# Wider spacing of the pieces of a recurrent layer between matrix products, on one Trainium2 core

## The chip, the cores and the metric

The kernel runs on one core of a Trainium2 chip. The metric is the device time of one execution in microseconds (us); the kernel before took 2150.6 us, the median of three runs (2145.4 to 2152.1). All engines below are those of the one core: PE (TensorE, matrix products and transposes), PEld (its loading of weights, which overlaps the products), DVE (VectorE), ACT (ScalarE), POOL (GpSimd) and SP (SyncE, which here issues the transfers).

## The reference

The program is a two-layer decoder trunk on 1024 tokens of width 1024, all in float32. The first layer mixes tokens by a gated linear recurrence (HGRN2), the second by attention in a sliding window of 128; each is followed by a gated feed-forward part with a short convolution (width 2816), and each part ends in `layer_norm(ALPHA * h + part)`. The change touches the recurrence. Cut to what matters, it is:

```python
q, f, i, g = jnp.split(h @ w_in, 4, axis=-1)            # w_in: 1024 x 4096, eight heads of 128
fg = lb + (1.0 - lb) * jax.nn.sigmoid(heads(f))
o = hgrn2_chunkwise(jax.nn.silu(heads(q)), 1.0 - fg, heads(i), jnp.log(fg))
    # S_t = diag(f_t) S_{t-1} + k_t v_t^T ;  o_t = S_t^T q_t
o = o * lax.rsqrt(jnp.mean(jnp.square(o), -1, keepdims=True) + RMS_EPS)
o = o * g_norm_w.astype(jnp.float32) * jax.nn.silu(heads(g))
return o.reshape(B, S, D).astype(h.dtype) @ w_out       # then layer_norm(ALPHA * x + ...)
```

So for each head there are four columns of projections (f, q, value, gate), a causal product whose scores carry the decay between two tokens, a state that is handed on from block to block of 128 tokens, a norm, a gate, and last the output projection over all heads.

## The kernel before, in words

**Arithmetic.** A float32 product is made of three fast ones, `mm3` (lines 173, 174, 175): each operand is split into a high part, which ACT casts (lines 154, 200, 811), and a low part, which DVE gets by a subtraction (line 147). Products with 512 columns into PSUM run back to back on PE for most of the program. PSUM holds four tiles `psmm` for the big products and two tiles `psax`, each of two banks, for everything else; whoever asks for a third `psax` waits until a tile has been read out.

**The stages.** (1) The input x comes in eight blocks of 128 tokens; PE turns each (`x_block`), ACT casts the high part, DVE subtracts, and ACT copies the turned block in full into the buffer `XF[tb]` for sums that are made later (lines 931 and 932). In between, the values of heads 0 and 1 and then the f, q and gate of head 0 are projected. (2) Thirteen "pairs" of columns (head 1's f and q, the gates of heads 1 and 2, f and q of head 2, the values of heads 2 and 3, and so on) are computed by a Strassen-like scheme: seven products of four `mm3` steps (twelve matmuls) each instead of eight (`product`), so 84 matmuls a pair. Three of the seven read sums of blocks of x (`SX`, called `sx` in the rows) on the right-hand side of SBUF, the others read `T` or sums in `HL`. The weights of each are loaded by SP, summed by DVE (lines 993 to 1009), and split. (3) Head 7's gate, the output projection (`out_part`, `out_proj`), the feed-forward part, then the second layer.

**The chain of a head.** While stage 2 runs, a generator `recur(h)` computes one head after the other in pieces. The pieces of a head are: on DVE the element-wise products r0, qp, r1 and r2 (lines 1187, 1188, 1190, 1194); on PE column sums of them and the first scores (line 179, tiles `St`, `kd`, `og`, `qp`, `kp`), which DVE places into `Ab` by mask (line 1141); scores over blocks of 8 and 16, with copies into `A` by ACT; wide scores over 32 and 64 tokens; the transposes of the keys (line 183, copied by ACT at line 1241); V times keys, which gives the states `St` (lines 1255, 1257); A times V plus states times q, then squares on ACT (line 1270), a power on POOL (lines 1271 and 1272) and the normed output `og` on DVE (line 1273); and the transposes of `og`, which DVE multiplies by the gate (line 1279) and SP writes to DRAM (`hod`). Between the scores, the queries and keys are scaled level by level (`update`): queries by DVE (line 1173), keys by POOL (line 1175) but for level 0, factors by DVE (line 1181). `turn_values` transposes the values of two heads (line 1124 is the copy).

**What sets the order.** PE and SP take their instructions in the order in which the program is written. The object `od` writes it: each `mm3` step advances a modelled clock, and each `yield n` in a generator means that its next piece is emitted when that clock has gone on by n us, so that matrix products lie between two pieces. DVE, ACT and POOL are ordered by a scheduler at build time; `urgent()` moves an instruction ahead there. A generator that waits on `state[...]` emits nothing until another has set it. What the yields are today, for heads 1 to 6:

```python
5.0   # og's transposes of the head before are out -> column sums and first scores
4.2   # -> scores over 8 and 16
4.2   # -> wide scores
2.2   # -> transposes of the keys
2.2   # -> V times keys
2.6   # -> A times V
8.0   # -> transposes of og
```

The time in the trace is not that of the model: on the chip one product of 512 columns follows the other after 0.22 to 0.23 us (the trace shows products at 219.80 and 220.02 us).

## Time and profile before

| | before |
|---|---|
| three runs | 2150.6, 2152.1, 2145.4 us |
| profiled execution: its time, its span | 2147.4 us, 2145.6 us |
| mean granted clock of PE | 0.996 |
| busy share: PE, PEld, DVE, ACT, POOL | 98%, 81%, 79%, 46%, 9% |
| recurrent layer with its heads | about 0 to 500 us |

The span runs from the first to the last instruction of the profiled execution. A timeline row gives start, duration, engine, line, operation, the tile written and the tile read, and in brackets the idle time ahead of it and what ended it. A row of the waits gives engine, tile, line, what was waited for, then total us, times, and the longest. A row of the windows gives the stretch, its length, busy time of each engine with the number of instructions, the granted clock (1.00 is full speed), the busy share of the DMA engines and GB/s.

### The profile page before, as it was taken

What the parts mean: (1) busy time and instruction counts of PE and PEld (TensorE: products, weight loads), DVE (VectorE), ACT (ScalarE), POOL (GpSimd) and SP (SyncE); (2) the same over time, 40 slices, a digit from 0 to 9 for tenths busy, and PEclk for the clock granted to TensorE, in tenths of its full rate; (3) what the DMA queues carried; (4) which work ended last, traced back from release to release, by engine and by line L of the source; (5) the groups of instructions that cost most, each with busy time, mean ns of one, the idle gap of its engine ahead of it and who ended that gap; (6) DMA issues with size and microseconds to landing.
All of it is one profiled execution on the core that took longest, in us unless ns stands there. A gap on an engine that the chain in (4) does not pass through costs nothing.

```text
span 2145.6 us, 32017 instructions
## 1 busy us (share of the span) xinstructions
PE 2104.6 (98%) x12511; PEld 1746.0 (81%) x12511; DVE 1690.5 (79%) x2282; ACT 994.5 (46%) x1586; POOL 202.6 (9%) x194
## 2 busy tenths in 40 slices
PE   9999999899999999999999999999999999999998
PEld 8888777778888888888888888888888888888886
DVE  6677666767988888887988546769988888887986
ACT  6454444442454444444433246743644444444430
POOL 1122122121100000000001123311000000000002
PEclk9999999999999999999999999999999999999999
DMA  4111111243243455547854311231244445559662
GB/s 152 40 50 48 33 50 54 76 152 108 98 130 110 147 164 167 167 138 268 301 192 167 116 35 36 62 138 72 85 158 138 154 144 163 167 170 314 229 225 99
DMA packets 268643, 285.25 MB, mean 133 GB/s; under 512 B 32073, under 2 KB 204874, under 8 KB 268234
## 3 DMA queue, kind: packets, MB, share of 16 engines
q1 hardware_dynamic: 267976, 283.06, 40.0%
q8 instruction: 98, 1.61, 0.3%
q14 instruction: 55, 0.45, 0.1%
q10 hardware_dynamic: 450, 0.12, 0.0%
q0 software_dynamic: 64, 0.02, 0.0%
HBM read 217.06 MB, written 66.09 MB: 132 GB/s over the span
## 4 chain that ended last, share of the span: by engine, by line
PE 75%; DVE 13%; DMA 7%; ACT 2%; issue 2%; SPq 1%; POOL 1%; DVEq 0%; ACTq 0%; POOLq 0%
PE psmm L173 15%; PE psmm L174 15%; PE psmm L175 15%; PE psax L173 8%; PE psax L175 7%; PE psax L174 7%; PE psax L179 3%; DVE HL L147 3%; DMA Y<-in_ffn_w_out_dram 2%; PE psmm L179 1%; PE psax L1528 1%; PE psax L183 1%; PE psmm L183 1%; DMA bsd<-Y 1%; DVE T L147 1%
## 5 line engine op out<-in xcount | busy, mean ns | idle before, releaser
L200 ACT CAST HL<-raw 128x1024 fp32r<-128x1024 f32 (+1 forms) x194 | 195.0, 1009 | 284.1 <-DVE raw L430 125.2
L173 PE MATMUL psmm<-T,HL 128*128 128x512 f32 x784 | 311.5, 397 | 0.9 <-ACT Y L494 0.8
L175 PE MATMUL psmm<-T,HL 128*128 128x512 f32 x784 | 305.9, 390 | 1.6 <-DVE HL L147 1.6
L174 PE MATMUL psmm<-T,HL 128*128 128x512 f32 x784 | 305.8, 390 | 0.1
L147 DVE TENSOR_TENSOR HL<-raw,HL 128x1024 fp32r<-128x1024 f32 (+1 forms) x218 | 258.5, 1189 | 56.1 <-ACT HL L200 28.6
L560 DVE SCALAR_TENSOR_TENSOR Y<-Y,cwt 128x1022 f32<-128x1022 f32 (+1 forms) x176 | 225.0, 1281 | 33.7 <-ACT Y L557 32.2
L222 POOL TENSOR_TENSOR rs<-rs,nhalf 128x1 f32<-128x1 f32 x32 | 46.0, 1439 | 1400.9 <-DVE rs L221 1400.9
L175 PEld LDWEIGHTS psmm<-T,HL 128*128 128x128 f32 x784 | 147.3, 188 | 33.7 <-DVE HL L147 2.1
L173 PEld LDWEIGHTS psmm<-T,HL 128*128 128x128 f32 x784 | 147.5, 188 | 32.0 <-ACT Y L494 2.1
L174 PEld LDWEIGHTS psmm<-T,HL 128*128 128x128 f32 x784 | 147.5, 188 | 29.7 <-DVE T L147 1.0
L173 PE MATMUL psax<-T,HL 128*128 128x512 f32 x352 | 137.9, 392 | 2.6 <-ACT Y L494 2.6
L175 PE MATMUL psax<-T,HL 128*128 128x512 f32 x352 | 137.1, 389 | 0.0
L174 PE MATMUL psax<-T,HL 128*128 128x512 f32 x352 | 137.0, 389 | 0.0
L557 ACT ACTIVATE Y<-Y,cwt 128x1024 f32<-128x1024 f32 x88 | 109.3, 1244 | 9.2 <-DVE Y L480 3.7
L454 DVE TENSOR_TENSOR Y<-Y 128x256 f32<-128x256 f32 x176 | 74.4, 423 | 44.7 <-DMA Y<-in_ffn_w_out_dram 42.7
L173 PE MATMUL psmm<-HL 128*128 128x512 f32 x216 | 86.7, 402 | 1.1 <-ACT G L1082 1.1
L174 PE MATMUL psmm<-HL 128*128 128x512 f32 x216 | 85.3, 395 | 0.0
L175 PE MATMUL psmm<-HL 128*128 128x512 f32 x216 | 85.2, 394 | 0.0
L173 PEld LDWEIGHTS psax<-T,HL 128*128 128x128 f32 x352 | 66.0, 188 | 17.5 <-ACT Y L494 4.1
L564 ACT ACTIVATE Y<-Y 128x1024 f32<-128x1024 f32 x44 | 46.5, 1061 | 71.2 <-DVE Y L560 71.2
L175 PEld LDWEIGHTS psax<-T,HL 128*128 128x128 f32 x352 | 66.1, 188 | 13.9
L174 PEld LDWEIGHTS psax<-T,HL 128*128 128x128 f32 x352 | 66.1, 188 | 13.5
(428 smaller groups left out, 5250.4 us busy)
## 6 DMA issues: line engine op xcount, KB each, us to landing
raw<-in_ffn_w_in_dram SPq DMA_DIRECT2D x136, 256.0 KB
raw<-gd SPq DMA_DIRECT2D x118, 256.0 KB
gd<-Y SPq DMA_DIRECT2D x44, 512.0 KB
Y<-in_ffn_w_out_dram SPq DMA_DIRECT2D x88, 256.0 KB
bsd<-Y SPq DMA_DIRECT2D x88, 256.0 KB
raw<-in_hgrn_w_in_dram SPq DMA_DIRECT2D x54, 256.0 KB
raw<-in_ffn_w_out_dram SPq DMA_DIRECT2D x54, 256.0 KB
R<-bsd SPq DMA_DIRECT2D x44, 256.0 KB
```

Source lines behind the costliest of these rows:

```text
L147: make = lambda e: e.tensor_tensor(lo, src, hi.bitcast(F32), op=ALU.subtract)
L173: nc.tensor.matmul(ps, st(0), mv(0), start=start, stop=False, **free)
L174: nc.tensor.matmul(ps, st(0), mv(1), start=False, stop=False, **free)
L175: nc.tensor.matmul(ps, st(1), mv(0), start=False, stop=stop, **free)
L179: nc.tensor.matmul(ps, lhsT, rhs, start=start, stop=stop, **kw)
L183: nc.tensor.transpose(ps, src, ident)
L200: nc.scalar.copy(hi, src)
L222: nc.gpsimd.tensor_tensor(rs, rs, nhalf, op=ALU.pow)
L454: tt(x, y, z, op=sub)
L557: nc.scalar.activation(c, u, AF.Identity, bias=cwt[:, l, 3, ci:ci + 1], scale=cwt[:, l, 2, ci:ci + 1])
L560: nc.vector.scalar_tensor_tensor(c[:, sh:], u[:, :S - sh], cwt[:, l, 2 - sh, ci:ci + 1], c[:, sh:], op0=ALU.mult, op1=ALU.add)
L564: nc.scalar.activation(c, c, AF.Silu)
```

## The change

The edits, in the order of the program:

- A tile `rpad` of 32 bytes in each partition is put first on the right-hand side of SBUF, so all that lies there (X, the sums SX, the tiles RA and Y) moves by 32 bytes: their addresses were 32 over a multiple of 64 and are now multiples of 64.
- While x is turned, the full copies of blocks 0 to 3 are made by DVE instead of ACT. Of blocks 4 to 7 ACT copies one half, and DVE makes the two sums of the block there (they were made later, at lines 931 and 932).
- The gates rotate through three tiles `gt0` to `gt2` instead of `Gx`, `G0`, `G1`.
- The yields between a head's pieces become a table `SP`; the pieces of `turn_values` come earlier (0.5, 1.5, and 1.5 more before the value counts as turned), and its copy and that of the keys are `urgent`.
- The transposes of the convolution's weights and the bias (`conv_params`) go into one `psax` tile and leave it in two copies; there were five tiles, each with its copy, with yields between them.
- The last head scales its keys on DVE, keeps r2 in a gate tile, and shares one `psax` tile from the transposes of the keys on; its first DVE pieces are emitted during head 6's last yield. The output projection's tiles 4 and 5, which lie in the other `psax`, begin once its wide scores are emitted (before: once its norm is). Tiles 0 to 3 of that projection go through heads 0 to 3 first and then heads 4 to 6; the heads' outputs 4 to 6 are loaded back later.

The diff, cut to its core:

```diff
+    ctx.enter_context(tc.tile_pool(name="rpad", bufs=1, side="right")).tile([P, 8], F32, name="rpad")
...
-                nc.scalar.copy(XF[tb], ps)
+                if tb < 4:
+                    copies[tb] = ps
+                    if tb:
+                        x_copy(tb)
+                else:
+                    a21, s1 = XF[tb][:, :512], XF[tb][:, 512:]
+                    nc.scalar.copy(a21, ps[:, :512])
+                    tt(s1, a21, ps[:, 512:], op=add)
+                    tt(a21, XF[tb - 4][:, :512], a21, op=sub)
+
+            copies = {}
+
+            def x_copy(tb):
+                nc.vector.tensor_copy(XF[tb], copies[tb])
...
                 us.append(split_into(hl_at(3), raw1).rearrange("p h (k c) -> p h k c", k=4))
+                x_copy(0)
...
             yield 12.0
-            for l, k, cr in crs:
-                ps = psax()
-                nc.tensor.transpose(ps[:, :88], cr, ident[:88, :88])
-                nc.vector.tensor_copy(cwt[:, l, 2 * k:2 * k + 2, :], ps[:, :88].rearrange("p (a b) -> p a b", a=2))
-                yield 1.0
             ps = psax()
-            nc.tensor.matmul(ps[:16, :2 * P], rb, oh, start=True, stop=True)
+            for i, (l, k, cr) in enumerate(crs):
+                nc.tensor.transpose(ps[:, 88 * i:88 * i + 88], cr, ident[:88, :88])
+            nc.tensor.matmul(ps[:16, 512:512 + 2 * P], rb, oh, start=True, stop=True)
+            nc.vector.tensor_copy(cwt.rearrange("p a b c -> p (a b c)"), ps[:, :4 * 88])
...
-            tt(s1, a21, s1, op=add)
-            tt(a21, a11, a21, op=sub)
...
-                    dest[n] = [hp.tile([P, S], F32, name=f"G{(h + i) % 2}") for i in range(2)]
+                    dest[n] = [hp.tile([P, S], F32, name=f"gt{(h + i) % 3}") for i in range(2)]
...
-                yield (0.5, 3.0)[e]
+                yield (0.5, 1.5)[e]
...
-                nc.scalar.copy(v, ps.rearrange("p (c t) -> p c t", c=NB))
+                with urgent():
+                    nc.scalar.copy(v, ps.rearrange("p (c t) -> p c t", c=NB))
+                yield 1.5
                 state["values"] = h + e
...
+            SP = {0: (7.5, 4.4, 4.4, 2.8, 2.8, 3.2, 8.0), NH - 1: (7.0, 4.2, 4.2, 2.4, 2.6, 2.6, 8.0)}.get(
+                h, (7.0, 5.0, 5.0, 2.8, 2.8, 3.2, 8.0))
...
+            def again():
+                if h < NH - 1:
+                    return psax()
+                if not kept:
+                    kept.append(psax())
+                return kept[0]
...
-                    (nc.gpsimd if i else nc.vector).tensor_tensor(view(nk, 0), view(k, 0),
+                    (nc.gpsimd if 0 < i and h < NH - 1 else nc.vector).tensor_tensor(view(nk, 0), view(k, 0),
...
-            yield {0: 7.5, NH - 1: 8.0}.get(h, 5.0)
+            yield SP[0]
...
-            nc.scalar.copy(kd, ps)
+            with urgent():
+                nc.scalar.copy(kd, ps)
...
-                yield from recur(h, *weights["out"].pop(h))
+                task = tasks.pop(h, None) or recur(h, *weights["out"].pop(h))
+                for wait in task:
+                    while h == NH - 2 and state["summed"] == h and wait > 0 and not tasks:
+                        if state["projected"] > h:
+                            tasks[h + 1] = recur(h + 1, *weights["out"].pop(h + 1))
+                            next(tasks[h + 1]), next(tasks[h + 1])
+                        else:
+                            yield 0.6
+                            wait -= 0.6
+                    yield wait
...
-        for tb in range(4):
-            begun.append(psmm())
-            out_part(begun[tb], us, tb, range(KC - 1))
+        begun = [psmm() for _ in range(4)]
+        for hs in (range(4), range(4, KC - 1)):
+            for tb in range(4):
+                out_part(begun[tb], us, tb, hs)
...
-        while state["summed"] < NH - 1:
+        while state["wide"] < NH - 1:
             od.step(chain)
```

How the change moves instructions is shown at three places. In the rows, a name with a number (`raw_92`) is one of several tiles of that name.

**DVE, where head 3 ends and head 4 begins.** The products that a head starts with (St, qp, kd, then og, which is r2) stand here behind the gating of the head before and behind low parts of weights (HL). Before:

```order
L1279 SCALAR_TENSOR_TENSOR G_2117<-psax,par,G_2117 128x1024
L147 TENSOR_TENSOR HL<-raw_92,HL 128x2x512
L1089 TENSOR_TENSOR qs<-qs,psmm 128x512
L147 TENSOR_TENSOR HL<-raw_93,HL 128x512
L1181 TENSOR_TENSOR tot<-tot 128x128
L1187 TENSOR_TENSOR St<-qs,kp 128x1024
L1188 TENSOR_TENSOR qp<-qs,fg 128x1024
L1181 TENSOR_TENSOR tot<-tot 128x64
L1190 TENSOR_TENSOR kd<-kp,qp 128x512
L997 TENSOR_TENSOR raw_93<-raw_92 128x512
L1173 TENSOR_TENSOR qp<-qp,fg 128x512
L1175 TENSOR_TENSOR kp<-kp,fg 128x512
```

And now:

```order
L1298 TENSOR_TENSOR og<-psax,ss 128x1024
L1210 TENSOR_TENSOR St<-qs,kp 128x1024
L1211 TENSOR_TENSOR qp<-qs,fg 128x1024
L1213 TENSOR_TENSOR kd<-kp,qp 128x512
L1196 TENSOR_TENSOR qp<-qp,fg 128x512
L1198 TENSOR_TENSOR kp<-kp,fg 128x512
L1304 SCALAR_TENSOR_TENSOR gt_2076<-psax,par,gt_2076 128x1024
L1217 TENSOR_TENSOR og<-kp,qp 128x512
L147 TENSOR_TENSOR HL<-raw_91,HL 128x2x512
L1096 TENSOR_TENSOR V<-V,psmm 128x512
```

The new head's first five operations stand directly behind the norm of the head before (line 1298, which was 1273) and ahead of its gating (line 1304, which was 1279).

**PE, the values of heads 6 and 7.** The eight transposes of a value (`ident,V`) and the seven products of values and keys (`V,kd`). Before:

```order
L175 MATMUL psmm<-sx_514,HL 128x512
L183 MATMUL psax<-ident,V 128x128 x8
L179 MATMUL psax<-V,kd 128x128 x7
L173 MATMUL psmm<-sx_514,HL 128x512
L174 MATMUL psmm<-sx_514,HL 128x512
```

And now:

```order
L179 MATMUL psax<-qp,kp 32x32 x32
L179 MATMUL psax<-St,kd 32x32 x32
L173 MATMUL psmm<-T,HL 128x512
L174 MATMUL psmm<-T,HL 128x512
L175 MATMUL psmm<-T,HL 128x512
L183 MATMUL psax<-ident,V 128x128 x8
L173 MATMUL psmm<-T,HL 128x512
```

The transposes stood directly ahead of the products that read their copy; they now stand behind the scores over 8 and 16, 27 matmuls of 512 columns or more ahead of those readers.

**ACT, at the start, while x is turned.** Casts of turned blocks (line 811, now 812), full copies (line 813) and the cast of the second half of the first weights (`HL<-raw_92`). Before:

```order
L833 COPY warm<-nhalf 128x1
L811 CAST T<-psax 128x8x128
L813 COPY kp<-psax 128x1024
L154 CAST HL<-raw_92 128x1024
L811 CAST T<-psax 128x8x128
L813 COPY og<-psax 128x1024
```

And now:

```order
L847 COPY warm<-nhalf 128x1
L812 CAST T<-psax 128x8x128
L154 CAST HL<-raw_92 128x1024
L812 CAST T<-psax 128x8x128 x3
L782 COPY V<-psmm 128x2x2x128
```

The cast of the weights now follows the first block's cast directly, and the full copies of the first four blocks are gone from ACT.

## The prediction

> **What bounds the kernel now.** I read the busy table of the page first, then PE's windows by stage, then PE's waits in the heads' stage, then the timeline around those waits.

> ```profile
> span 2145.6 us, 32017 instructions
> PE 2104.6 (98%) x12511; PEld 1746.0 (81%) x12511; DVE 1690.5 (79%) x2282; ACT 994.5 (46%) x1586; POOL 202.6 (9%) x194
> ```

> PE is busy for 98% of the span: over the whole only 41.0 us are idle, so a change that takes no PE work away can return little more than that, plus what the clock costs. The windows tell where the idle time lies (busy time, granted clock, DMA share, GB/s):

> ```profile
> 0.00:20.00 20.00, 16.04 (x108) 1.00 0.93 326
> 60.00:120.00 60.00, 59.10 (x546) 1.00 0.13 39
> 120.00:200.00 80.00, 78.35 (x907) 1.00 0.17 52
> 200.00:300.00 100.00, 93.65 (x966) 0.98 0.18 54
> 300.00:400.00 100.00, 92.46 (x790) 0.97 0.15 46
> 400.00:500.00 100.00, 94.89 (x918) 1.00 0.35 127
> ```

> From 60 to 500 us, where the heads run, PE is busy 418.45 of 440 us: 21.55 us idle, half of the program's. The clock is below 1.00 only in two of these windows. What the idle time of 60 to 500 us waited for (total, times, longest):

> ```profile
> PE psax L179 <- POOL kp L1175: 4.3, 3, 1.8
> PE psax L179 <- ACT V L1124: 4.0, 3, 1.7
> PE psax L179 <- DVE Ab L1141: 3.7, 4, 1.8
> PE psax L179 <- DVE og L1194: 2.6, 2, 1.6
> PE psax L907 <- DVE G L1279: 1.7, 1, 1.7
> PE psmm L175 <- DVE HL L147: 1.6, 1, 1.6
> PE psax L179 <- DVE tot L1181: 1.2, 1, 1.2
> PE psmm L173 <- ACT G L1082: 1.1, 1, 1.1
> PE psax L179 <- DVE qp L1173: 0.9, 1, 0.9
> ```

> These rows sum to 21.1 us, so they are nearly all of the idle time: each wait is a piece of a head that PE reaches before DVE, ACT or POOL has made its input. Every wait also costs a little more than it shows:

> ```profile
> 220.02 0.39 PE L174 MATMUL psmm<-T,HL 128*128 128x512 f32 x1
> 220.25 0.39 PE L175 MATMUL psmm<-T,HL 128*128 128x512 f32 x1
> 221.78 0.50 PE L173 MATMUL psmm<-HL 128*128 128x512 f32 x1 [1.15 <-ACT G L1082]
> ```

> One product lasts 0.39 us but the next begins 0.23 us after it, so each restart loses an overlap of 0.16 us that counts as busy.

> **The change, part by part.** The sum is made against the profiled execution, 2147.4 us (span 2145.6), 3.2 us under the median.

> *Pieces spread wider.* No PE work is added or removed by the yields; between a head's pieces there lie three matmuls more (0.68 us at 0.227 us each) ahead of the scores, the wide scores, and V times keys, and the column sums come 45 matmuls behind the last head's transposes (10.2 us) instead of 36 to 39 (8.2 to 8.9; heads 5 and 7 had 57). Further, DVE now makes the new head's r0, qp and r1 ahead of the gating of the last one and of low parts of weights, and so earlier against PE by those operations (the order of DVE shows them). The rows `kp`, `og` and `tot` (8.1 us) are at the sums and first scores; 1.3 to 2.0 us later and an earlier DVE cover waits of at most 1.8 us each. I leave 0.5 us at head 7, whose spacing of the scores stays 4.2: 7.6. `Ab` (3.7 us, four times, up to 1.8): the scores' 0.68 us and the wide scores' 0.68 us follow one another, so 1.36 us each, and I take 3.2. `V` (4.0 us): the transposes stood directly ahead of V times keys, or close to the wide scores; now 27 or more matmuls (6.1 us) lie between them and the copy's reader, and the longest wait was 1.7, so all 4.0 goes. `G L1279` (1.7) is a chain of five turned convolution weights through `psax`, now one: it goes. `G L1082` (1.1) is ACT's copy of a gate, held by the writing of that gate tile's last content to DRAM:

> ```profile
> 221.15 0.59 ACT L1082 COPY G<-psmm 128x512 f32<-128x512 f32 x1 [3.52 <-DMA hod<-G]
> ```

> With a third tile that transfer has another pair's time (84 matmuls, 19 us); it goes. Of `HL` (1.6 us, once) I take 1.0: DVE's queue is another there, and nothing was done for it. `qp` (0.9) stays: head 0's spacing ahead of its sums doesn't move. Sum: 7.6 + 3.2 + 4.0 + 1.7 + 1.1 + 1.0 = 18.6, and 15 restarts at 0.16 make 2.4: **-21.0 us** (0 to 24.1: all 21.55 and 16 restarts).

> *The clock.* Twice PE ran at half clock after two such waits in a row:

> ```profile
> 277.95 0.64 PE L179 MATMUL psax<-og,one 128*32 128x256 f32 x8 [1.05 <-DVE og L1194]
> 279.82 1.08 PE L179 MATMUL psax<-qp,kp 128*32 128x32 f32 x64 [1.23 <-DVE tot L1181]
> ...
> 337.04 0.64 PE L179 MATMUL psax<-og,one 128*32 128x256 f32 x8 [1.58 <-DVE og L1194]
> 338.91 1.08 PE L179 MATMUL psax<-qp,kp 128*32 128x32 f32 x64 [1.23 <-POOL kp L1175]
> ...
> 279.90:283.10 3.20, 3.20 (x69) 0.50 0.02 5
> 338.00:344.00 6.00, 5.09 (x74) 0.50 0.01 3
> ```

> Half of the busy time of these stretches is the loss, (3.20 + 5.09) / 2 = 4.1 us at most. Both stretches begin behind waits of 2.3 and 2.8 us in all, and from 400 to 500 us, with 5.1 us of waits, the clock is 1.00. I take **-3.6** (0 to -4.1), since the four waits are among those that go. [...]

> *The start.* ACT's full copies stand ahead of the casts that PE and DVE wait for:

> ```profile
> 8.95 1.02 ACT L813 COPY kp<-psax 128x1024 f32<-128x1024 f32 x1 [1.29 <-DVE T L147]
> 9.86 1.05 ACT L154 CAST HL<-raw 128x1024 fp32r<-128x1024 f32 x1
> 10.96 0.39 PE L173 MATMUL psmm<-HL,T 128*128 128x256 f32 x1 [0.53 <-ACT HL L154]
> 12.22 0.39 PE L174 MATMUL psmm<-HL,T 128*128 128x256 f32 x1 [0.88 <-DVE HL L147]
> 25.05 0.39 PE L175 MATMUL psmm<-HL,T 128*128 128x256 f32 x1 [0.82 <-DVE T L147]
> ```

> Block 0's copy (1.02 us) no longer precedes the cast of the weights, so 0.53 and 0.88 go; the third wait stands behind DVE, which gets four copies but loses nothing it needs before. I take 2.2 of waits and 0.3 of restarts: **-2.5** (-1.0 to -2.7, all three with restarts). DVE's copies cost the path nothing as long as blocks arrive slower than DVE turns them: the DMA engines are 0.93 busy in 0 to 20 us.

> *The shift by 32 bytes.* Products that read `sx` as the moving side are a little longer than those that read `T`:

> ```profile
> L174 PE MATMUL psmm<-T,HL 128*128 128x512 f32 x247 | 96.4, 390 | 0.0
> L174 PE MATMUL psmm<-sx,HL 128*128 128x512 f32 x104 | 41.0, 395 | 0.0
> ```

> Of this form there are three lines of 104. If the address is what makes 395 of 390, the change returns 312 x 5 ns = **-1.6**; if it is the tile, 0. Nothing else tells `sx` from `T` in these rows, so I take 1.6.

> *What it costs.* (1) At heads 1, 3 and 5 only six matmuls (1.36 us) lie between the wide scores and the keys' transposes, which need the last scaling of the keys by POOL:

> ```profile
> 140.53 1.52 POOL L1175 TENSOR_TENSOR kp<-kp,tot 128x512 f32<-128x512 f32 x1 [3.99 <-PE psax L179]
> ```

> 1.52 us, and a start, against 1.36 and the wide scores' own time beyond the last read: some 0.5 each, +1.5 (0 to 3). (2) In the order of DVE at even heads a sum of weights that waits for a transfer stands among the placements that give PE's scores tile back. The nearest row is this wait:

> ```profile
> 300.90 0.69 DVE L997 TENSOR_TENSOR raw<-raw 128x512 f32<-128x512 f32 x1 [2.08 <-DMA raw<-in_hgrn_w_in_dram]
> ```

> Behind DVE stand then the placements, and PE's next scores wait for them. By the modelled spacing there is slack but for some 0.4 us; I take 0.5 at heads 2, 4 and 6: +1.5 (0 to 6.3, the whole 2.08 three times). (3) Head 7's keys are scaled by DVE:

> ```profile
> 449.56 0.69 DVE L1175 TENSOR_TENSOR kp<-kp,fg 128x512 f32<-128x512 f32 x1
> 434.00:497.00 63.00, 61.16 (x560) 50.69 (x559) 40.13 (x61) 27.35 (x57) 12.34 (x8) 1.00 0.35 129
> 497.00:560.00 63.00, 63.00 (x299) 52.53 (x298) 61.66 (x92) 21.82 (x32) 10.29 (x7) 1.00 0.28 98
> ```

> Six of them are 4.1 us (the third column is DVE); from 434 to 497 us DVE has 23 us free, so they hide, and cost 4.1 if that cover is gone. POOL's six leave a chain in which DVE and POOL handed over to each other, which is part of the gain of the `kp` row and already in it. (4) Head 7's last transposes come six matmuls, not fifteen, ahead of the first product with its output, so the gating is some 2.0 us later against PE; DVE is full from 497 to 560 us (61.66 of 63), so what is late there is late once more at its end, where PE today waits

> ```profile
> 585.93 0.50 PE L174 MATMUL psmm<-TX,HT 128*128 128x512 f32 x1 [0.37 <-DVE TX L147]
> ```

> a little already. I take +1.5 (0 to 2.2: the 2.0 and a restart). In all +4.5 (0 to 15.6). The feed-forward part and the second layer hold the same instructions: 0.

> Sum: -21.0 - 3.6 - 2.5 - 1.6 + 4.5 = **-24.2 us**, 2147.4 - 24.2 = 2123.2 for a profiled execution. The median lay 3.2 over the profile, so I say **2124 us**, 1.2% under the median.

> **The rivals.**

> *The half clock stays* (15%). If it falls by a count of its own and not by these waits, the 3.6 us are not returned: 2147.4 - 20.6 = 2126.8, about 2127 to 2128. [...] Against it speaks that both stretches begin within 1 us of a second wait.

> *Half the gain moves on* (14%). DVE and ACT take their queues in order; a piece that comes later for PE also ends later for the piece behind it, and 1.36 us more per pair of pieces may only move a wait to V times keys or to the norm, for which yields grew by 0.6 each. What speaks for it: of the handovers between engines in a head the rows show only those that end last. What speaks against it: DVE has 23 of 63 us free, and eight heads take 440 us, 55 each, of which PE is busy 52, so products and not the chain set the pace. Half of 24.2 returned: about 2136.

> *It does nothing* (6%): the end is set elsewhere, say by DVE in 497 to 560 us, full at 61.66 of 63. Everything that PE gains before 497 us would then be waited for at the feed-forward part's begin. Against it: DVE has free time before and its input there comes from PE. 2145 to 2150.

> *Slower, by the transfer in DVE's queue* (7%). The subtraction that waits for weights now stands before the placements at every head. If it waits 2.1 us there (the row at 300.90), the scores and the wide scores both wait, 4.2 us, and two such waits bring the half clock once more, 3.4 / 2 = 1.7 us: 5.9 us at seven heads is 41 us, 2147.4 - 24.2 + 41 = about 2164. It decides from 24.2 / 7 = 3.5 us a head. For it: transfers of weights are started when a split frees their tile, and DVE is now earlier against PE, not the transfer. Against: at odd heads that subtraction stands behind the placements, and the transfers have 0.15 to 0.18 of the DMA engines in this stage.

> **How the numbers follow.** Main case 58%, own range 2115 to 2132 (all gains and no cost would be 24.1 + 4.1 + 2.7 + 1.6 = 32.5, thus 2115; costs of twice my estimate and 4 us less gain are 2132). The range for 8 in 10 takes in the second case and half of the third: 2114 to 2140. Some 0.3%, 6.5 us, is what a measurement of this kernel can tell from no change. Faster by more than that: main case, half clock and the second, 58 + 15 + 14 = 87%, of which 1 goes to within, for a half that comes out smaller: 86%; within: 6 + 1 = 7%; slower: 7%.

> **What would show it.** In the profile of the changed kernel: PE idle in the heads' stage below 8 us; the clock 1.00 in all windows (if not, the first rival); no `V`, `og` or `G` among PE's waits; `sx` products at 390 ns (if 395, the shift did nothing); the cast of the first weights directly behind block 0's cast, and PE's first waits there gone; short waits for `kp` ahead of the keys' transposes at heads 1, 3 and 5. A wait for DVE behind a transfer at even heads speaks for the last rival, longer waits for `TX` near 585 us for cost (4). I am wrong if PE's idle time in the heads' stage stays above 12 us, or if it falls and the time doesn't.

## The result, and the profile after

The changed kernel took **2121.4 us** (median of four runs, 2116.6 to 2124.7) against 2149.6 us for the kernel before (four runs): ratio 0.9869, 95% interval 0.9843 to 0.9895. The prediction was 2124 us, range 2114 to 2140. A second set of runs beside the kernel before gave 2122.2 us and 0.9878 (0.9851 to 0.9905), e12 below. The profiled execution of the changed kernel, from which the rows here are taken, is the slowest of its four (2124.7 us).

The page's head of the changed kernel answers to the two lines of before:

```profile
span 2122.9 us, 31989 instructions
PE 2099.1 (99%) x12511; PEld 1746.8 (82%) x12511; DVE 1697.2 (80%) x2289; ACT 987.9 (47%) x1582; POOL 198.3 (9%) x188
```

The span is 22.7 us shorter. PE's busy time fell by 5.5 us and its idle time from 41.0 to 23.8 us, that is by 17.2. PE's windows by stage (us, busy time with instructions, granted clock, DMA share, GB/s), first of the changed kernel:

```profile
0.00:40.00 40.00, 37.29 (x281) 1.00 0.56 192
60.00:500.00 440.00, 435.69 (x4228) 1.00 0.22 72
500.00:560.00 60.00, 58.21 (x289) 1.00 0.26 94
620.00:2110.00 1490.00, 1483.13 (x7345) 1.00 0.47 155
```

and the same stretches of the kernel before:

```profile
0.00:40.00 40.00, 34.91 (x264) 1.00 0.56 190
60.00:500.00 440.00, 418.44 (x4121) 0.99 0.20 66
500.00:560.00 60.00, 60.00 (x286) 1.00 0.28 97
620.00:2110.00 1490.00, 1484.31 (x7354) 1.00 0.48 156
```

In the heads' stage PE's idle time fell from 21.56 to 4.31 us, at the start by 2.38 us; from 500 to 560 us it rose by 1.79. The rest of the program stands as it was (1.2 us more idle from 620 us on, inside the scatter there: 3.2 to 8.5 us of idle time in the profiles below). The clock is 1.00 in the heads' stage; the mean over the program lies a little lower, at 0.998, for one stretch at half clock near 920 us (last section). What is left of the waits there, and the new one behind it, in the waits of the changed kernel (60 to 500 us, then 500 to 700):

```profile
PE psax L179 <- DVE St L1282: 2.5, 1, 2.5
PE psax L179 <- DVE qp L1196: 0.9, 1, 0.9
PE psax L183 <- POOL kp L1198: 0.6, 3, 0.2
...
PE psmm L174 <- DVE T L147: 1.8, 1, 1.8
PE psmm L174 <- DVE TX L147: 0.4, 1, 0.4
```

Of the eighteen waits of before one is left as it was (`qp`, head 0); with one of 0.2 us for `Ab` there are six in all. The waits for `kp` now stand ahead of the keys' transposes (line 183) and are 0.2 us each. The wait for `St` is new. DVE's timeline of the changed kernel shows whose it is:

```profile
361.35 0.69 DVE L1008 TENSOR_TENSOR raw<-raw 128x512 f32<-128x512 f32 x1 [3.06 <-DMA raw<-in_hgrn_w_in_dram]
361.96 0.34 DVE L1282 SCALAR_TENSOR_TENSOR St<-St,tot,psax 128x128 f32<-128x128 f32 x1
```

In the middle of head 5's chain of states stands a sum of weights (line 1008, which was 997) that waits 3.06 us for its transfer, and the rest of the chain waits behind it in DVE's queue. This is the mechanism of the prediction's cost (2) and of its last rival, at another piece and at one head, an odd one where the prediction had the even ones.

### The profile page after: what moved, and what is told of

Same layout as the page of the kernel before. It is cut to its first block, busy times and chain, and to the rows that moved or that the text cites. A ratio compares the mean times of both kernels' runs of the same rounds, so it can differ in the third digit from the quotient of the medians.

```text
span 2122.9 us, 31989 instructions
## 1 busy us (share of the span) xinstructions
PE 2099.1 (99%) x12511; PEld 1746.8 (82%) x12511; DVE 1697.2 (80%) x2289; ACT 987.9 (47%) x1582; POOL 198.3 (9%) x188
## 4 chain that ended last, share of the span: by engine, by line
PE 78%; DVE 11%; DMA 7%; issue 2%; ACT 2%; POOL 0%; SPq 0%; DVEq 0%; ACTq 0%; POOLq 0%
PE psmm L173 16%; PE psmm L174 16%; PE psmm L175 16%; PE psax L173 8%; PE psax L174 8%; PE psax L175 8%; PE psax L179 3%; DVE HL L147 2%; DMA Y<-in_ffn_w_out_dram 2%; PE psax L183 1%; PE psmm L179 1%; DVE T L147 1%; DMA bsd<-Y 1%; PE psax L1562 1%; PE psmm L183 1%
## 5 line engine op out<-in xcount | busy, mean ns | idle before, releaser
L200 ACT CAST HL<-raw 128x1024 fp32r<-128x1024 f32 (+1 forms) x194 | 194.3, 1008 | 289.6 <-DVE raw L430 125.9
L173 PE MATMUL psmm<-T,HL 128*128 128x512 f32 x784 | 311.8, 398 | 1.1 <-ACT Y L494 1.0
L147 DVE TENSOR_TENSOR HL<-raw,HL 128x1024 fp32r<-128x1024 f32 (+1 forms) x218 | 256.3, 1183 | 65.7 <-ACT HL L200 40.3
L174 PE MATMUL psmm<-T,HL 128*128 128x512 f32 x784 | 305.9, 390 | 1.9 <-DVE T L147 1.8
L175 PE MATMUL psmm<-T,HL 128*128 128x512 f32 x784 | 306.1, 390 | 0.0
L173 PEld LDWEIGHTS psmm<-T,HL 128*128 128x128 f32 x784 | 147.4, 188 | 31.8 <-ACT Y L494 2.2
L174 PEld LDWEIGHTS psmm<-T,HL 128*128 128x128 f32 x784 | 147.5, 188 | 31.4 <-DVE T L147 2.7
L175 PEld LDWEIGHTS psmm<-T,HL 128*128 128x128 f32 x784 | 147.2, 188 | 31.4
L173 PE MATMUL psax<-T,HL 128*128 128x512 f32 x352 | 138.6, 394 | 2.6 <-ACT Y L494 2.5
L174 PE MATMUL psax<-T,HL 128*128 128x512 f32 x352 | 137.8, 392 | 0.0
L175 PE MATMUL psax<-T,HL 128*128 128x512 f32 x352 | 137.7, 391 | 0.0
L173 PE MATMUL psmm<-HL 128*128 128x512 f32 x216 | 85.0, 393 | 0.0
L175 PE MATMUL psmm<-HL 128*128 128x512 f32 x216 | 84.2, 390 | 0.0
L174 PE MATMUL psmm<-HL 128*128 128x512 f32 x216 | 84.1, 390 | 0.0
L173 PEld LDWEIGHTS psax<-T,HL 128*128 128x128 f32 x352 | 66.5, 189 | 17.5 <-ACT Y L494 3.8
L175 PEld LDWEIGHTS psax<-T,HL 128*128 128x128 f32 x352 | 66.5, 189 | 13.9
L174 PEld LDWEIGHTS psax<-T,HL 128*128 128x128 f32 x352 | 66.5, 189 | 13.5
```

The lines of the kernel that those rows point to most:

```text
L147: make = lambda e: e.tensor_tensor(lo, src, hi.bitcast(F32), op=ALU.subtract)
L173: nc.tensor.matmul(ps, st(0), mv(0), start=start, stop=False, **free)
L174: nc.tensor.matmul(ps, st(0), mv(1), start=False, stop=False, **free)
L175: nc.tensor.matmul(ps, st(1), mv(0), start=False, stop=stop, **free)
L200: nc.scalar.copy(hi, src)
```

## The experiments

Each kernel is the kernel before, or the changed one, with the edit shown. Idle time and clock are read from one profile each, PE's window from 60 to 500 us; a time without an interval is one run and tells little below 5 us.

**e1: yields and gate tiles alone, on the kernel before.** The yields without the third gate tile were not tried.

```diff
+            SP = {0: (7.5, 4.4, 4.4, 2.8, 2.8, 3.2, 8.0), NH - 1: (7.0, 4.2, 4.2, 2.4, 2.6, 2.6, 8.0)}.get(
+                h, (7.0, 5.0, 5.0, 2.8, 2.8, 3.2, 8.0))
...
-                    dest[n] = [hp.tile([P, S], F32, name=f"G{(h + i) % 2}") for i in range(2)]
+                    dest[n] = [hp.tile([P, S], F32, name=f"gt{(h + i) % 3}") for i in range(2)]
```

Expected:

> The kernel before with two parts of the change alone: the table of yields and the three gate tiles (nothing else; values, start, convolution weights, last head as before). Theory A, spacing itself covers the heads' waits: PE's waits for kp, og, tot and Ab (11.8 us before) fall under 2 us, the wait for the gate's copy (1.1) goes, no window shows a clock under 1.00; the waits for V (4.0) and for the convolution weights (1.7) stay. That is 10.8 + 1.1 + 1.9 of restarts + 3.6 to 4.1 of clock, some 18 us: about 2131 us, ratio 0.992. Rival B, half of it moves on (V times keys and the states' chain start later against nothing): idle time from 60 to 500 us falls by less than 7 us, about 2141.

Measured: 2136.7 us, ratio 0.9934 (0.9917 to 0.9951), 14 us less than before; idle 12.6 us in the heads' stage. Its window and its waits:

```profile
60.00:500.00 440.00, 427.40 (x4183) 0.99 0.22 71
...
PE psax L183 <- DVE og L1275: 5.8, 1, 5.8
PE psax L179 <- DVE St L1259: 2.9, 1, 2.9
PE psax L179 <- DVE Ab L1143: 1.1, 1, 1.1
PE psax L179 <- DVE qp L1175: 0.9, 1, 0.9
```

Theory A holds for six heads: the waits for `kp`, `og` and `tot` at the sums and scores are gone, and so is the one for the gate's copy; `Ab` is left with 1.1 us and 0.7 more ahead of the transposes of the keys. Two things were not expected. The waits for V (4.0 us) went as well, without the edit of the values. And at the end of head 6 there is a new wait of 5.8 us with half clock (0.50 from 426 to 432 us): the chain now ends later than the products that it is laid between, and the transposes of the normed output come directly behind the products that make it (PE's timeline):

```profile
422.29 0.39 PE L179 MATMUL psax<-St,qp 128*128 128x128 f32 x2
428.43 1.97 PE L183 MATMUL psax<-ident,og 128*128 128x128 f32 x8 [5.76 <-DVE og L1275]
```

So rival B, that a part of the gain moves on, is right in kind for the spacing by itself: the 8.7 us of `og` and `St` are waits that were not there. Its size is not met: idle time fell by 9.0 us and not by less than 7.

**e2: the changed kernel with the old yields.**

```diff
-            SP = {0: (7.5, 4.4, 4.4, 2.8, 2.8, 3.2, 8.0), NH - 1: (7.0, 4.2, 4.2, 2.4, 2.6, 2.6, 8.0)}.get(
-                h, (7.0, 5.0, 5.0, 2.8, 2.8, 3.2, 8.0))
+            SP = {0: (7.5, 4.2, 4.2, 2.2, 2.2, 2.6, 8.0), NH - 1: (8.0, 4.2, 4.2, 2.2, 2.2, 2.6, 8.0)}.get(
+                h, (5.0, 4.2, 4.2, 2.2, 2.2, 2.6, 8.0))
```

> The changed kernel with the yields of before (5.0, 4.2, 4.2, 2.2, 2.2, 2.6, 8.0; head 0 7.5, head 7 8.0 first), all else as changed. Theory A: the waits for kp, og, tot and Ab come back with some 8 to 12 us and with them at least one stretch at half clock: about 2121 + 14 to 18 = 2135 to 2139. Rival C, the gain sits in the order of DVE, in the values' transposes and in the last head: PE's idle time from 60 to 500 us stays under 8 us and the time under 2126.

Measured: 2146.2 us, ratio 0.9986 (0.9974 to 0.9997). The window, and the largest of its waits:

```profile
60.00:500.00 440.00, 421.08 (x4123) 0.98 0.21 67
...
PE psax L179 <- DVE og L1217: 5.0, 3, 2.1
PE psax L179 <- DVE Ab L1156: 3.6, 4, 1.2
PE psax L179 <- POOL kp L1198: 3.0, 3, 1.2
PE psmm L173 <- DVE qs L1096: 1.8, 1, 1.8
```

18.9 us idle, and three stretches at half clock. Without the yields all the other parts together return 3 to 4 us; with them 28. Theory A holds, more strongly than expected (25 us instead of 14 to 18): rival C falls. The two single studies give 14 and 4 us (the gate tiles are in both), the whole 28, so some 10 us belong to neither part alone; the seam at head 6 in e1 (5.8 us and the clock behind it) is the largest single wait in it.

**e3: the new copies of x alone, on the kernel before.**

```diff
-                nc.scalar.copy(XF[tb], ps)
+                if tb < 4:
+                    copies[tb] = ps
...
+                    tt(a21, XF[tb - 4][:, :512], a21, op=sub)
```

> The kernel before with the changed copies of x alone (blocks 0 to 3 by DVE, sums of blocks 4 to 7 there). Prediction's step: the waits of 0.53, 0.88 and 0.82 us go, PE's busy time from 0 to 40 us rises from 34.9 to 37.2 us or more, the rest of the profile is that of before: some 2.5 us less, which one look can't tell by its time. Rival: DVE's copies delay the low parts, and the busy time stays.

Measured: 2147.8 us in one run, which tells nothing by itself; busy time from 0 to 40 us 37.28 us, up 2.37 from 34.91, and the heads' stage as before:

```profile
0.00:40.00 40.00, 37.28 (x279) 1.00 0.56 191
60.00:500.00 440.00, 418.31 (x4119) 0.99 0.20 66
```

The step is as predicted, and it stands alone: 2.4 us.

**e4: the values' earlier transposes alone, on the kernel before.**

```diff
-                yield (0.5, 3.0)[e]
+                yield (0.5, 1.5)[e]
...
+                with urgent():
+                    nc.scalar.copy(v, ps.rearrange("p (c t) -> p c t", c=NB))
+                yield 1.5
```

> The kernel before with the earlier transposes of the values and their urgent copies alone. Prediction's step: the three waits for V (4.0 us) go and the other waits stay as they are: idle time from 60 to 500 us 21.6 - 4.0 = 17.6 us, 4.5 us less in time. Rival: the waits are handed on to the next piece (states, norm), idle time stays over 20 us.

Measured: 2158.6 us in one run, 8.4 us over the median before where 4.5 us less were expected; idle 20.5 us in the heads' stage, one less than before. From its window and waits:

```profile
60.00:500.00 440.00, 419.47 (x4109) 0.98 0.20 64
...
PE psmm L173 <- DVE qs L1085: 1.8, 1, 1.8
PE psax L179 <- ACT V L1125: 1.6, 1, 1.6
```

The waits for V fell from 4.0 to 1.6 us, but a wait of 1.8 for `qs` took the place of most of it: the rival is right here. The same wait of 1.8 stands in e2, the other kernel that has this edit and the old yields. The longer time is not idle time: this profile has seven stretches at half clock of 3.4 us each (the profile before has one of 3.4 and one of 6.8), and two of them stand behind waits of 1.85 us for `Ab` and `kp` that the kernel before has with 1.83 and 1.84, without half clock behind them (last section).

**e5: waits of growing length, on the changed kernel.**

```diff
-            for j in range(2):
+            for j in [0, 1] * ({1: 4, 2: 5, 3: 6, 4: 7, 5: 8, 6: 9}.get(h, 1)):
                 nc.vector.tensor_tensor(r2[:, j], kp[:, j::4].unsqueeze(2).to_broadcast([P, S // 4, 2]),
```

> The changed kernel with r2 of heads 1 to 6 computed 4, 5, 6, 7, 8 and 9 times over instead of once (the same values, 1.25 us of DVE each time), so that PE waits once a head ahead of the r2 sums, for longer at each head: by a slack of some 4 us about 0, 1, 2, 3, 4.5 and 6 us. What it is for: how long a wait halves the clock. By the two stretches of before (waits of 2.3 and 2.8 us in all within 4 us) theory A expects half clock from a wait of about 2 us on, so at heads 3 to 6. [...] The time is some 15 to 25 us over the changed kernel's.

Measured: 2177.1 us in one run, some 55 over the changed kernel and not 15 to 25. The ladder did not have the rungs that it was made for. Behind each wait for r2 came a second one for the keys' scaling by POOL, so PE was idle for 3.4, 4.6, 5.7, 7.0, 8.1 and 8.9 us at the six heads, and all six were followed by half clock. Head 1, the shortest:

```profile
130.78 1.08 PE L179 MATMUL psax<-qp,kp 128*32 128x32 f32 x64 [3.44 <-POOL kp L1198]
...
130.00:134.00 4.00, 3.22 (x69) 0.50 0.56 159
```

It says that 3.4 us and more halved the clock each time; it does not say what a wait of 2 us does, for which the other kernels have to serve (last section).

**e6: head 7's gate earlier, on the changed kernel.**

```diff
-            SP = {0: (7.5, 4.4, 4.4, 2.8, 2.8, 3.2, 8.0), NH - 1: (7.0, 4.2, 4.2, 2.4, 2.6, 2.6, 8.0)}.get(
+            SP = {0: (7.5, 4.4, 4.4, 2.8, 2.8, 3.2, 8.0), NH - 1: (7.0, 4.2, 4.2, 2.4, 2.6, 2.6, 5.5)}.get(
```

> The changed kernel with head 7's last yield 5.5 instead of 8.0: the transposes of its normed output stand 12 matmuls (2.7 us) earlier. Theory A (cost 4 of the prediction: the late gate makes DVE late for the feed-forward part): PE's new wait of 1.8 us for T near 548 us goes, about 2 us less than the changed kernel, 2119 to 2120. Rival E: DVE is the bound from 480 us on by its own amount of work, whatever it starts with: the wait stays over 1 us and the time within 1 us of the changed kernel's.

Measured: 2119.5 us, ratio 0.9862 (0.9845 to 0.9878), which can't be told from the changed kernel's. The wait near 548 us is 0.87 us in place of 1.79:

```profile
547.81 0.50 PE L174 MATMUL psmm<-T,HL 128*128 128x512 f32 x1 [0.87 <-DVE T L147]
```

But in the six profiles with the gate late (the changed kernel, e7 to e10 and e12) the same wait is 0.9 to 1.9 us, so the halving isn't shown to be due to the edit (e11, which has it too, shows 0.8). That DVE is full there is: from 470 to 560 us it is busy 87.61 of 90 in the changed kernel. Between theories A and E this stays open.

**e7: head 7's keys on POOL again, on the changed kernel.**

```diff
-                    (nc.gpsimd if 0 < i and h < NH - 1 else nc.vector).tensor_tensor(view(nk, 0), view(k, 0),
+                    (nc.gpsimd if i else nc.vector).tensor_tensor(view(nk, 0), view(k, 0),
```

> The changed kernel with head 7's keys scaled on POOL again, the other five parts of the last head as changed. Theory A: the scaling that took 3.85 us on POOL before stands between the sums and the first scores, so a wait for kp of 2 to 3.5 us is back at head 7, later pieces of head 7 as changed: idle time from 400 to 500 us 2 to 4 us over the changed kernel's 0.1. Rival: it hides, nothing moves.

Measured: 2125.6 us; idle from 60 to 500 us 5.8 us, and of it from 400 to 500 us 1.2 (the changed kernel: 0.1). The largest waits, `St` (1.4) and `qp` (0.9) left out:

```profile
PE psax L179 <- DVE Ab L1156: 1.8, 2, 1.5
PE psax L179 <- POOL kp L1198: 0.6, 1, 0.6
PE psax L179 <- ACT kd L1266: 0.6, 1, 0.6
```

Of these only the 0.6 us for `kp`, at 431 us, is head 7's; the one for `kd` stands at 411 us in head 6, and the longer one for `Ab` at 185 us in head 2, both untouched by the edit. So what came back is 0.6 us and not 2 to 3.5: theory A has the place and not the size. DVE's six extra operations in the changed kernel cost nothing that shows, as predicted.

**e8: the changed kernel without the 32 bytes.**

```diff
-    ctx.enter_context(tc.tile_pool(name="rpad", bufs=1, side="right")).tile([P, 8], F32, name="rpad")
```

> The changed kernel without the tile of 32 bytes. The changed kernel's profile still has 395 ns for products that read sx, so the prediction's 1.6 us is expected to be no effect: sx products at 395 ns here too, time within 1 us of the changed kernel's. Rival: the shift acts elsewhere (evacuation into Y, casts) and its loss shows as 2 us or more.

Measured: 2124.7 us, ratio 0.9887 (0.9872 to 0.9902), inside the intervals of the changed kernel's two sets, though 2.5 and 3.3 us over their medians, where at most 1 was expected. Products that read `sx`, without the tile; in the changed kernel the row is the same, and before it said 41.0 and 395:

```profile
L174 PE MATMUL psmm<-sx,HL 128*128 128x512 f32 x104 | 41.1, 395 | 0.0
```

The address is not what makes 395 of 390 ns. What does is open. Its profile has one stretch at half clock, near 550 us, behind a wait of 1.89 us for `T` that the changed kernel has with 1.79. An effect of some 3 us elsewhere, the rival, isn't excluded.

**e9 and e10: the seam at head 6.** e9 puts back one step, which the list of edits in the section on the change leaves out: head 7's sums are emitted ahead of head 7's gate products, as before. e10 takes the early beginning of head 7 away.

```diff
+            while state["first"] < NH - 1:
+                od.step(chain)
             GT[NH - 1] = hp.tile([P, S], F32, name="gt1")
...
-            while state["first"] < NH - 1:
-                od.step(chain)
             heads = [hp.tile([P, S], F32, name=n) for n in ("fg", "qs")]
```

```diff
-                for wait in task:
-                    while h == NH - 2 and state["summed"] == h and wait > 0 and not tasks:
...
-                    yield wait
+                yield from task
```

> The changed kernel with one step of the last head put back: head 6's end and head 7's first sums are emitted ahead of the gate products of head 7, as before, and not behind them; all else as changed. Theory F: with the wide yields head 6's chain needs these products between its pieces; without them A times V, norm and the transposes of og follow each other on PE and it waits for ACT, POOL and DVE in a row: one wait of 4 to 6 us near 420 us, as in the kernel with yields and gates alone, and half clock behind it (some 3 us): 7 to 9 us over the changed kernel, 2129. Rival: the wait is not there, the time as changed.

> The changed kernel without the early beginning of head 7 during head 6's last yield; head 7 begins when head 6 is done. Theory F: the gate products of head 7 alone close the seam at head 6, and the early beginning covers only DVE's first products of head 7: a wait of 0 to 3 us for og or kp at head 7's sums, no wait for the transposes of head 6: 0 to 4 us over the changed kernel. Rival: the early beginning is what closes the seam: 5 to 6 us of wait there.

Measured: e9 2122.5 us with 4.9 us idle in the heads' stage, among it one wait of 1.2 us for `kp` at head 7; no wait at head 6. e10 2131.0 us, with 8.2 us idle and half clock twice, once of it at the place shown here (the other near 363 us, behind the wait for `St`). From the waits of e10, and the timeline behind its largest:

```profile
PE psax L183 <- DVE og L1298: 3.6, 1, 3.6
PE psax L179 <- DVE St L1282: 1.5, 1, 1.5
PE psmm L173 <- ACT T L200: 1.0, 1, 1.0
...
469.70 0.40 PE L175 MATMUL psax<-HL,T 128*128 128x512 f32 x1
473.65 1.09 PE L183 MATMUL psax<-ident,og 128*128 128x128 f32 x8 [3.56 <-DVE og L1298]
475.75 0.79 PE L173 MATMUL psmm<-HL,T 128*128 128x512 f32 x1 [1.01 <-ACT T L200]
```

Theory F was wrong for e9, where its rival holds. For e10 it was right that the seam at head 6 stays closed, and wrong on what the early beginning covers. Taking either step away doesn't bring the 5.8 us of e1 back; a kernel without both was not tried, so which edit closes the seam at head 6 isn't shown. What the early beginning covers is the other end: without it head 7 ends too late, the output projection runs out of products (470 us), and PE waits 3.6 us for head 7's norm, then 1.0 for the cast of its output, then runs at half clock.

**e11 and e12: a version meant to be better, beside the changed kernel.**

```diff
-            SP = {0: (7.5, 4.4, 4.4, 2.8, 2.8, 3.2, 8.0), NH - 1: (7.0, 4.2, 4.2, 2.4, 2.6, 2.6, 8.0)}.get(
-                h, (7.0, 5.0, 5.0, 2.8, 2.8, 3.2, 8.0))
+            SP = {0: (7.5, 4.4, 4.4, 2.8, 2.8, 3.2, 8.0), NH - 1: (7.0, 4.2, 4.2, 2.4, 2.6, 2.6, 5.5)}.get(
+                h, (7.0, 5.0, 5.0, 2.8, 2.8, 4.2, 7.0))
```

> The changed kernel with head 7's last yield at 5.5 and, for heads 1 to 6, the last two yields at 4.2 and 7.0 instead of 3.2 and 8.0 (the products of A and V come 1.0 us later, the transposes of og at the same place). The wait for St at one head (2.5, 1.0, 0.8 us in the profiles so far) goes, the wait for T near 548 us is about halved: 1 to 3 us under the changed kernel, 2118 to 2120. Rival: the later norm makes the gate and the next head's first DVE products late, and a wait for og or kp is back: 2 us or more over it.

> The changed kernel once more, beside the one above on the same chip: 2119 to 2123 us, ratio to before 0.985 to 0.989. Its profile should again show no window at 0.50 between 60 and 500 us; a stretch near 0.57 without a wait ahead of it may be anywhere or missing.

Measured: 2122.3 us (0.9868, 0.9846 to 0.9889) and 2122.2 us (0.9878, 0.9851 to 0.9905): no difference. The wait for `St` is gone in e11, as expected, but others came: 1.4 us in three waits for V, and 0.4 more each for `Ab` and `kp`. Idle time in the heads' stage is 4.5 us, against 3.6 in e12. No version was shown to beat the changed kernel.

## Why the prediction was right, point by point

The forecast of 24.2 us less was met by 22.7 us in the span and 28 us in the medians of these runs. The terms, by the profile of the changed kernel, a minus being a gain:

| term | predicted | measured | from |
|---|---|---|---|
| waits in the heads' stage | -21.0 | -19.7, cost (2) left out | idle 21.56 to 4.31, and 2.5 of the rest is cost (2); restarts below |
| half clock | -3.6 | -4.6, and 1.7 back elsewhere | no window at 0.50 from 60 to 500 us; half clock from 918.3 to 921.7 us |
| start | -2.5 | -2.4 | 34.91 to 37.29 busy of 40; e3: 37.28 |
| 32 bytes | -1.6 | 0 | 395 ns with and without (e8) |
| cost (1), `kp` ahead of transposes | +1.5 | +0.6 | three waits of 0.2 |
| cost (2), transfer in DVE's queue | +1.5 | +2.5 | one wait for `St` of 2.5 |
| cost (4), late gate | +1.5 | +1.8 | wait for T near 548 us |

The idle time of 4.31 us holds costs (1) and (2); in the first row only (2) is taken out, so the cost (1) of 0.6 is counted in it. Twelve waits fewer also give back their overlaps of 0.16 us, 1.9 us, which the first row does not hold either. The prediction read 4.1 us at most for the clock from two narrow windows; by the granted clock the stretches of before run from 279.80 to 283.22 and from 337.83 to 344.66 us, PE is busy for 3.40 and 5.75 us of them, and half of that is 4.6. PE's busy time should then have fallen by 4.6 - 1.7 + 1.9 = 4.8 us; it fell by 5.5, and 0.7 us is not assigned. Without counting cost (1) twice the measured terms sum to -19.7 - 1.9 - 4.6 + 1.7 - 2.4 + 2.5 + 1.8 = -22.6 us, against 22.7 in the span. That the forecast of -24.2 lies so near is partly luck: the waits and restarts gave 2.1 us more than their row and cost (1) together, while the 32 bytes, the clock and costs (2) and (4) came out 3.6 worse.

- **The bound.** Right: PE's idle time was where the waits of the heads were, and hardly anywhere else did the time move.
- **The spacing.** Right in size. e2 shows that the yields are the condition of nearly all of it: 25 us go without them. The step on V was wrong in its reason: the transposes' new place by itself gave 1.0 us of idle time and not 4.0, since a wait for `qs` came in its stead (e4); the yields took V's waits away without it (e1).
- **What the prediction did not see** is that the wider chain overruns its products at the last two heads. It put the last head's edits down as costs that hide and as a late gate. e1 and e10 show what such edits have to cover: 5.8 us at head 6's end and 3.6 + 1.0 at head 7's, each with half clock behind it. The sum came out because the changed kernel as a whole leaves neither wait, which the prediction did not ask about.
- **The clock.** Right: the stretches went with their waits, and the first rival falls. No profile of the changed kernel (e12's is a second one) or of e6, e7, e8, e9 and e11 has a window at 0.50 between 60 and 500 us; e10 has two, behind its waits for `St` and `og`. Half clock came with pairs of waits of 2.3 and 2.8 us in all, as the prediction read the trace of before, and in eight of twelve cases behind a single wait of 1.77 to 1.89 us (last section).
- **The 32 bytes.** Wrong: the term of 1.6 us was put on a difference of 5 ns that stays when the address is changed back.
- **Costs.** (1) was over-sized, three waits of 0.2 us. (2) was the right mechanism, at the states of head 5 instead of the scores of heads 2, 4 and 6. (3) hides, as said. (4) has the size that was given and not the place: the wait for `TX` near 585 us, named as its sign, stayed at 0.4, and the new wait is for `T` near 548 us. e6 leaves open whether the late gate or DVE's load makes it.
- **The rivals.** "Half the gain moves on" is what the parts do by themselves (e1 and e4), not the whole. "Slower by the transfer in DVE's queue" occurred once, at 2.5 of the 3.5 us a head from which it would have decided. The 3.4 us of half clock that it halves is the length that the trace of before shows from 279.80 to 283.22 us; behind the wait of 2.5 us the clock stayed at 1.00.

## What to carry to other kernels

When an engine that is 98% busy waits in many short pieces for chains on other engines, more of its own work between the pieces can return these waits almost in full, as here (21.6 us of idle time became 4.3); but the chain gets longer, so look first at its last rounds, where the work to put in between runs out (5.8 us at head 6 in e1). Edits of that kind are worth little one by one: here 14 and 4 us for two parts that together are 28. In a queue that is taken in order, look for the instruction that waits for a transfer: here one sum of weights waited 3.06 us, the states behind it in DVE's queue waited too, and PE 2.5 us for them.

## What the runs showed of the hardware

**When the clock halves.** PE's idle time between two big products, in the profiles of all the kernels above from 60 to 620 us (the fourth kind to the end of the program), and what came next:

- 3.4 to 8.9 us: half clock all eight times (six in e5, one each in e1 and e10);
- two waits of 2.7 to 3.0 us in all, with small column sums between them: half clock all five times (before, e2 twice, e3, e4);
- such a pair of 2.2 to 2.3 us: half clock before and in e4, not in e2 and e3;
- one wait of 1.77 to 1.89 us: half clock eight times of twelve;
- one wait of 1.0 to 1.7 us: once in 39 (1.5 us for `St`, in e10);
- unlike the others, one wait of 2.5 us (changed kernel, for `St`) and one of 2.9 us (e1, for `St`): not.

The changed kernel itself has one of the fourth kind, far behind the change, at 916 us, where a wait of 1.83 us between big products is followed by 3.4 us in which a product comes every 0.43 us:

```profile
918.16 0.67 PE L173 MATMUL psax<-T,HL 128*128 128x512 f32 x1 [1.83 <-ACT Y L494]
918.63 0.63 PE L174 MATMUL psax<-T,HL 128*128 128x512 f32 x1
919.06 0.63 PE L175 MATMUL psax<-T,HL 128*128 128x512 f32 x1
...
921.62 0.46 PE L175 MATMUL psax<-T,HL 128*128 128x512 f32 x1
```

So here full clock followed a wait of 1.0 to 1.7 us in 38 of 39 cases, and the 1.83 us at 916 us cost 1.7 us more, the half of 3.4; whether a wait of this length does so differed from run to run of nearly the same program (eight of twelve).

```profile
358.54:361.95 3.41, 2.59 (x14) 1.00 0.17 48
361.95:365.37 3.42, 1.77 (x15) 1.00 0.00 0
```

PE was idle for 0.8 us in the one and 1.65 in the other. The wait of 2.9 us in e1 falls into windows with 1.2 and 1.74 us idle in the same way, the latter inside the span where both came out. The one exception of the 61 is the wait of 1.5 us in e10. What decides between 1.74 and 1.86 us is open; the ends of PE's operations in a trace are modelled.

**POOL beside DVE.** The same operation of POOL on the same shapes, the first scaling of the keys in place, took 1.6 us in the changed kernel at head 1 and 4.5 us in e5:

```profile
121.28 0.69 DVE L1007 TENSOR_TENSOR raw<-raw,raw 128x512 f32<-128x512 f32 x1
121.50 1.63 POOL L1198 TENSOR_TENSOR kp<-kp,tot 128x512 f32<-128x512 f32 x1 [11.21 <-DVE og L1217]
121.88 1.81 DVE L1196 TENSOR_TENSOR qp<-qp,tot 128x512 f32<-128x512 f32 x1
```

```profile
126.25 4.47 POOL L1198 TENSOR_TENSOR kp<-kp,tot 128x512 f32<-128x512 f32 x1 [16.01 <-DVE og L1217]
...
126.03 1.22 DVE L147 TENSOR_TENSOR HL<-raw,HL 128x1024 fp32r<-128x1024 f32 x1
127.17 0.68 DVE L1196 TENSOR_TENSOR qp<-qp,tot 128x512 f32<-128x512 f32 x1
127.77 1.82 DVE L147 TENSOR_TENSOR HL<-raw,HL 128x1024 fp32r<-128x1024 f32 x2
```

In both, POOL ends 1.1 to 1.2 us after an operation of DVE: in the first row set after the sum that ends at 121.97, in the second after the low parts that follow each other until 129.59. In the changed kernel DVE's next operation, which takes 0.68 us in e5 (127.17), takes 1.81 and ends 0.6 us after POOL (123.69 and 123.13). How many operations of DVE end before POOL does isn't regular: one in the first row set, four in the second. The same distance stands behind all 90 scalings of keys on POOL in the profiles before and after, counting DVE's `TENSOR_TENSOR` with both inputs outside PSUM (low parts, line 147, sums of weights and scalings alike): 85 end 0.91 to 1.18 us after the last of these that ended beside them, and the five beside which none ended take 1.05 to 1.16 us in all. DVE's `TENSOR_TENSOR` with an input in PSUM (`psmm`) that ran beside these scalings, 14 in the two profiles, took 0.67 to 0.69 us each. All of this is read from traces; no experiment was made on it, so the cause isn't shown.

The row of 3.85 us in the kernel before (451.62) is of this kind: the last of DVE's operations beside it ends at 454.33 us, 2.7 us after POOL's start, and POOL's ends 1.14 us later. Behind it stands the longest of the three waits for POOL before (1.84 us). The other two (1.23 us) stand behind operations of 1.70 us, which end 1.14 us after one of DVE's.
